# The score-times-value product of a gated linear attention in three fp32r passes instead of one fp32 product

## The chip, the cores and the metric

The kernel runs on one core of one Trainium2 chip. The metric is the time of one execution on the device in microseconds (us), the median of several runs. The profile is one more execution, taken by the hardware profiler. PE is the TensorE, DVE the VectorE, ACT the ScalarE, POOL the GpSimd, and SP the engine that issues most DMAs.

## What is computed

One layer of a decoder trunk on 256 tokens of width 2048, in float32. The normalised input is multiplied by a wide weight matrix. Its columns feed three branches: a causal convolution, a gated linear attention (GLA) and a cross-attention into 256 memory tokens. Each branch is projected back, gated, and the sum goes through an output matrix and a last RMSNorm.

The change is in the GLA. For each of four heads the reference does this, chunk by chunk over the tokens:

```
scores = einsum("bhtk,bhsk,bhtsk->bhts", qi, ki, decay)
o_intra = einsum("bhts,bhsv->bhtv", scores, vi)
o = o_inter + o_intra
```

The kernel does not carry a state. It builds the whole causal 256 x 256 score matrix of a head, decay included, as three blocks of 128 x 128, and multiplies it by v (256 tokens x 512): the first token block from one score block, the second from two.

## The kernel before, in words

**The large products.** All weight products go in three passes of upper and lower parts: a float32 number is split into `hi`, rounded to the PE's short float32 form (fp32r), and `lo`, the rest, also fp32r, and `mm3` (L180 to L183) adds hi x hi, hi x lo and lo x hi. Weights arrive in chunks of two 128-row blocks, 512 KB each; `chunk` (L150) issues the DMA on SP, ACT writes `hi` (L160) and DVE writes `lo` (L161). Four raw buffers and five pairs of hi and lo let this run ahead of the PE. `group_t` (L185) makes 512 output features x 256 tokens with 24 matmuls of 256 columns per chunk, `group_n` (L195) 256 tokens x 512 features with 12 matmuls of 512 columns per chunk.

**The order.** The program runs group after group: the first convolution group (ca0, cb0), q0, k0, va and vb (head 0's v and the small decay input), v1, ca1, cb1, q1, k1, v2, v3, ca2, cb2, mk, mv, mq, mz, then the gate and output groups (gm, ym, gz, go, yo, cz, gc, yc, out). Between chunks `tick` (L117) lets side tasks emit a few instructions: the convolution taps, the norms, and `gla_head` (L517) for each head. A planner then orders each engine's instructions, by its own estimate of durations and by priority, with the weight chunks preferred. On the chip every engine works its list strictly in that order.

**The head.** `gla_head` forms the scores over several levels (`pd`, `pl`), corrects the first block in `sT[:, 0]`, makes the cross block in `px` (L623) and turns the last block around in `pf` (L626). DVE copies those two from PSUM into `sX` (L624) and `s1` (L627). After a pause of two ticks the PE makes `po` (L635, L637, L638): three plain fp32 matmuls of 512 columns per head. ACT sums the squares (L641), POOL the scale, DVE writes the normalised result (L643).

**v.** `v_group` (L666) makes v in one 4 KB tile (per partition) per head; ACT copies it out of PSUM (L671, and L677 and L686 for head 0).

**Pools and offsets.** Tiles of 4 KB come from a pool of NB4 = 19, of 2 KB from NB2 = 7, of 1 KB from NB1 = 8. `KICKS` (L40) lists, per group, chunks whose second row block lies 64 bytes further on in the hi and lo buffers; nothing else depends on it:

```
lines = [1] * (ck - 1) + [2 if k // CK in shifted else 1]
...
first = LINE * at[0]
step = GC + LINE * (at[-1] - at[0])
```

Of the kernel before, what the change touches and what calls it, by code (L numbers as in the profile page):

```python
# [9 lines left out]
F32R = mybir.dt.float32r  # L10
# [6 lines left out]
P = 128  # L17
D = 2048
T = 256
NT = T // P  # L20
# [7 lines left out]
DVH = 512  # L28
# [2 lines left out]
RANK = 16  # L31
MEM_W = 512
MHD = 128
NB4, NB2, NB1, NRAW, NHL = 19, 7, 8, 4, 5
NU, LAG, HELD, XWAIT = 2, 2, 12, 8
WARM = 9
SPARE = 1.2
LINE, HLW = 16, CK * GC + P

KICKS = {"ca0": (0, 4), "cb0": (2,), "ca1": (0,), "cb1": (6,), "q1": (2, 4, 6, 7), "k1": (1, 5), "ca2": (0, 4),  # L40
         "cb2": (0, 3), "mk": (0, 2, 5), "mq": (5,), "mz": (1, 4, 7), "gm0": (0, 2, 3), "go0": (0, 4, 5),
         "go1": (3, 5), "yo1": (6,), "go2": (0,)}
AHEAD = 400
LEVELS = (1, 2, 4, 8, 16, 32, 64)

# [16 lines left out]
def trunk_kernel(ctx, tc, streamed, xt, memt, x, weights, w_alpha2, vecs, taps, b_gate, b_conv_out,  # L62
                 final_g, ident_in, masks_in, out):
    nc = tc.nc
# [6 lines left out]
    def mm_tile(name):  # L71
        return ps.tile([P, GC], F32, name=name, tag="mm", bufs=5)

    def aux_tile(name):
        return ps.tile([P, GC], F32, name=name, tag="aux", bufs=3)

    def b4(shape, name, dt=F32):
        return bp.tile(shape, dt, name=name, tag="b4", bufs=NB4)
# [4 lines left out]
    def t2(shape, name):  # L83
        return tp.tile(shape, F32, name=name, tag="t2", bufs=NB2)

    def t1(shape, name, dt=F32):
        return tp.tile(shape, dt, name=name, tag="t1", bufs=NB1)
# [8 lines left out]
    def start(gen, rank=1):  # L96

        task = [gen, 0, rank]
        at = len(Side.queue)
        while at and Side.queue[at - 1][2] > rank:  # L100
            at -= 1
        Side.queue.insert(at, task)
        return task
# [60 lines left out]
    def chunks(w, cols, nk, acts, name, first=CK, spare=False, shifted=None):  # L164
        if not isinstance(cols, list):
            cols = [(cols, GC)]
        k = 0
        while k < nk:
            ck = min(CK, first) if k < 2 * first else CK
            lines = None  # L170
            if shifted is not None:
                lines = [1] * (ck - 1) + [2 if k // CK in shifted else 1]
            hi, lo = chunk(w, k, ck, cols, f"{name}_{k}", spare and k + ck > nk - HELD and k < nk - 8, lines)
            ops = [acts(k + kk) for kk in range(ck)]
            for kk in range(ck):
                yield k + kk, hi[kk], lo[kk], *ops[kk]
            k += ck
            tick()

    def mm3(o, ah, al, bh, bl, first, last):  # L180
        nc.tensor.matmul(o, lhsT=ah, rhs=bh, start=first, stop=False, skip_group_check=True)  # L181
        nc.tensor.matmul(o, lhsT=ah, rhs=bl, start=False, stop=False, skip_group_check=True)  # L182
        nc.tensor.matmul(o, lhsT=al, rhs=bh, start=False, stop=last, skip_group_check=True)  # L183

    def group_t(w, c0, acts, nk, name, first=CK):  # L185

        pss = [mm_tile(f"pt_{name}_{j}") for j in range(2)]
        for k, hi, lo, ah, al in chunks(w, c0, nk, acts, name, first, shifted=KICKS.get(name, ())):
            for n in range(4):
# [5 lines left out]
    def group_n(w, c0, acts, nk, name):  # L195

        n = sum(c[1] for c in c0) if isinstance(c0, list) else GC
        pss = [mm_tile(f"pn_{name}_{t}")[:, 0:n] for t in range(NT)]
        for k, hi, lo, ah, al in chunks(w, c0, nk, acts, name):
            for t in range(NT):  # L200
                tok = slice(t * P, (t + 1) * P)
                mm3(pss[t], ah[:, tok], al[:, tok], hi, lo, k == 0, k == nk - 1)
        return pss

    def split(src, hi, lo):
        nc.scalar.copy(hi, src)
        nc.vector.tensor_sub(lo, src, hi.bitcast(F32))
# [9 lines left out]
    def rms_scale(ss, n, name, w=1):  # L217

        ms = tp.tile([P, w], F32, name=f"ms_{name}", tag="ms")
        nc.vector.tensor_scalar(ms, ss, 1.0 / n, EPS, op0=ALU.mult, op1=ALU.add)  # L220
        rs = tp.tile([P, w], F32, name=f"rs_{name}", tag="rs")
        nc.gpsimd.tensor_tensor(rs, ms, mhalf[:, 0:w], op=ALU.pow)
        return rs
# [292 lines left out]

    def gla_head(h, q, k, v):  # L517

        while len(cum) <= h:
            yield "wait", 1  # L520
        c = cum[h]
# [12 lines left out]
            return bass.AP(tensor=ap.tensor, offset=ap.offset + at, ap=[list(ap.ap[0]), *(list(x) for x in dims)])  # L534

        sT = t1([P, 2, P], f"sT{h}")
        sX = t1([P, P], f"sX{h}")
        s1 = t1([P, P], f"s1{h}")

        qq = b4([P, 4, P + CHUNK], f"qq{h}")  # L540
        d1 = t1([P, T], f"dq{h}_1")
# [11 lines left out]
        for i in range(2):  # L553
            for a in range(2):
                keys = k[:, a, 0:P] if i == 0 else ck[:, 3 * T + a * P:3 * T + (a + 1) * P]
                nc.tensor.matmul(pdv[:, i, :], lhsT=keys, rhs=qq[:, 2 * a + i, :],
                                 start=a == 0, stop=a == 1, skip_group_check=True)
# [63 lines left out]
        px = aux_tile(f"px{h}")  # L621
        for a in range(2):
            nc.tensor.matmul(px[:, 0:P], lhsT=kd[:, a, :], rhs=qd[:, a, :], start=a == 0, stop=a == 1)  # L623
        nc.vector.tensor_copy(sX, px[:, 0:P])  # L624
        pf = aux_tile(f"pf{h}")
        nc.tensor.matmul(pf[:, 0:P], lhsT=flip, rhs=sT[:, 1, :], start=True, stop=True)  # L626
        nc.vector.tensor_copy(s1, pf[:, 0:P])  # L627
        yield "wait", 2

        ov = b4([P, NT, DVH], f"on{h}")  # L630
        on[h] = ov
        for t in range(NT):
            po = aux_tile(f"po{h}_{t}")
            if t == 0:
                nc.tensor.matmul(po, lhsT=sT[:, 0, :], rhs=v[:, 0, :], start=True, stop=True)  # L635
            else:
                nc.tensor.matmul(po, lhsT=sX, rhs=v[:, 0, :], start=True, stop=False)  # L637
                nc.tensor.matmul(po, lhsT=s1, rhs=v[:, 1, :], start=False, stop=True)  # L638
            sq = t2([P, DVH], f"osq{h}_{t}")
            ss = tp.tile([P, 1], F32, name=f"oss{h}_{t}", tag="ss")  # L640
            nc.scalar.activation(sq, po, AF.Square, accum_out=ss)  # L641
            rs = rms_scale(ss, DVH, f"o{h}_{t}")
            nc.vector.tensor_scalar_mul(ov[:, t, :], po, rs)  # L643
            yield 0.7

    def qk_group(g, acts, rb=None):
        rbb = None if rb is None else rb.unsqueeze(1).to_broadcast([P, 2, T])
        pq = group_t("w_in", C_Q + g * GC, acts, KT, f"q{g}")
        q = b4([P, 4, T], f"q{g}")
        for j in range(2):  # L650
            qj = q[:, 2 * j:2 * j + 2, :]
            if rb is None:
                nc.scalar.activation(qj, pq[j], AF.Copy, scale=DKH ** -0.5)
            else:
                nc.vector.scalar_tensor_tensor(qj, pq[j], DKH ** -0.5, rbb, op0=ALU.mult, op1=ALU.mult)
        pk = group_t("w_in", C_K + g * GC, acts, KT, f"k{g}")
        k = b4([P, 4, T], f"k{g}")
        for j in range(2):
            kj = k[:, 2 * j:2 * j + 2, :]
            if rb is None:  # L660
                nc.scalar.copy(kj, pk[j])
            else:
                nc.vector.tensor_mul(kj, pk[j], rbb)
        return q, k

    def v_group(h, q, k):  # L666
        v = b4([P, NT, DVH], f"v{h}")
        if h:
            pv = group_n("w_in", C_V + h * DVH, X, KT, f"v{h}")
            for t in range(NT):  # L670
                nc.scalar.copy(v[:, t, :], pv[t])  # L671
        else:

            n = (DVH + RANK) // 2
            pv = group_n("w_in", [(C_V, n)], X, KT, "va")
            for t in range(NT):
                nc.scalar.copy(v[:, t, 0:n], pv[t])  # L677
            pv = group_n("w_in", [(C_V + n, DVH - n), (C_AL, RANK)], X, KT, "vb")
            alr = t1([P, NT, P], "alr")
            nc.gpsimd.memset(alr, 0.0)  # L680
            for t in range(NT):
                al = pv[t][:, DVH - n:n]
                nc.scalar.copy(alr[:, t, 0:RANK].bitcast(F32R), al)
                nc.vector.tensor_sub(alr[:, t, 32:32 + RANK].bitcast(F32R), al, alr[:, t, 0:RANK])
                nc.vector.tensor_copy(alr[:, t, 64:64 + RANK], alr[:, t, 0:RANK])
                nc.scalar.copy(v[:, t, n:DVH], pv[t][:, 0:DVH - n])  # L686
            start(decay(alr))
        s = slice(2 * (h % 2), 2 * (h % 2) + 2)
        return start(gla_head(h, q[:, s, :], k[:, s, :], v))


    def memory_groups():
# [172 lines left out]
    q, k = qk_group(0, XR, xrb)  # L865
    finish(norm)
    load_masks()
    gla = [v_group(0, q, k), v_group(1, q, k)]
    tapsk.append(conv_group(1, X))
    q, k = qk_group(1, X)  # L870
    gla += [v_group(2, q, k), v_group(3, q, k)]
    start(load_biases())
    mnorm = start(mem_norm(), rank=0)
# [43 lines left out]
    for n in range(3):  # L917
        po = group_n("w_out", n * GC, Y, KT, f"out{n}")
# [35 lines left out]
    for k, hi, lo, ah, al in chunks("w_out", 3 * GC, KT, Y, "out3", spare=True):  # L954
        mm3(pss[0], ah[:, 0:P], al[:, 0:P], hi, lo, k == 0, k == KT - 1)
        held.append((k, hi, lo, ah, al))
        if k < KT - HELD:
            k, hi, lo, ah, al = held.pop()
# [53 lines left out]
```

## Time and profile before

| what | value |
|---|---|
| median of 3 runs | 1223.62 us (1223.38 to 1223.81) |
| profiled execution, its own time | 1224.49 us |
| span of its instructions | 1222.6 us |
| granted PE clock, mean over the span | 0.999 |
| busy share PE, DVE, ACT, POOL | 99%, 77%, 49%, 2% |

The span is the time from the first to the last instruction; the execution's own time has a little more around it. Starts of matmuls are recorded; their ends are modelled and overlap, so the step from one start to the next, not the duration, is what a matmul costs in a stream. An fp32 matmul stands in the trace as two records.

### The profile page before, as it was taken

Reading aid. Unit: us, or ns where it says so; the run is one execution under the profiler, and the core shown is the slowest. Engines: PE = TensorE matmul, PEld = TensorE weight load, DVE = VectorE, ACT = ScalarE, POOL = GpSimd, SP = SyncE. Lnnn points to the kernel's source line nnn. Section 1 sums busy time; section 2 is a strip of 40 time slices with the busy share of each in tenths; the row PEclk is TensorE's granted clock in tenths of the full one; section 3 lists DMA queues with packets and bytes.
Section 4 is the critical chain, followed back from the end, with each engine's and each line's share of the span. In section 5 each row is a group of like instructions: output and inputs, shape, how many; then the busy total and the mean of one; then the engine's idle time right before and its main releaser. Section 6 shows DMA issues by size and latency. Waiting matters only on the chain.

```text
span 1222.6 us, 22810 instructions
## 1 busy us (share of the span) xinstructions
PE 1210.4 (99%) x9337; PEld 1156.4 (95%) x9337; DVE 938.0 (77%) x1479; ACT 598.1 (49%) x743; POOL 21.6 (2%) x32
## 2 busy tenths in 40 slices
PE   8999999999999999999999999999999999999997
PEld 8999899989998999999988999999999999999885
DVE  6999999699999667997699967974565554555553
ACT  6734666446553454444444445444354544444442
POOL 0000000100030000000000000000000000000000
PEclk9999999999999999999999999999999999999999
DMA  9666756457556545666565665566666666666862
GB/s 339 222 184 191 222 165 205 151 158 236 187 162 199 165 150 178 197 199 194 171 206 187 190 192 156 190 222 191 193 189 204 192 191 195 197 193 204 281 213 78
DMA packets 70488, 236.57 MB, mean 193 GB/s; under 512 B 8192, under 2 KB 12480, under 8 KB 70384
## 3 DMA queue, kind: packets, MB, share of 16 engines
q1 hardware_dynamic: 69952, 234.54, 61.2%
q8 instruction: 73, 1.20, 0.4%
q10 hardware_dynamic: 432, 0.58, 0.1%
q14 instruction: 31, 0.25, 0.1%
HBM read 232.99 MB, written 2.10 MB: 192 GB/s over the span
## 4 chain that ended last, share of the span: by engine, by line
PE 95%; DMA 2%; DVE 2%; issue 0%; ACT 0%; SPq 0%; POOL 0%; POOLq 0%; DVEq 0%; ACTq 0%
PE pt_go L181 2%; PE pt_gm L181 2%; PE pt_go L182 2%; PE pt_go L183 2%; PE pt_cz L182 2%; PE pt_yo L181 2%; PE pn_gz L182 2%; PE pt_yo L182 2%; PE pt_gc L182 2%; PE pn_gz L181 2%; PE pt_yc L183 2%; PE pn_out L181 2%; PE pn_out L183 2%; PE pn_gz L183 2%; PE pt_gm L182 2%; PE pt_yc L182 2%
## 5 line engine op out<-in xcount | busy, mean ns | idle before, releaser
L407 DVE SCALAR_TENSOR_TENSOR conv<-u,tap,conv 128x256 f32<-128x256 f32 x480 | 207.7, 480 | 0.0
L161 DVE TENSOR_TENSOR lo_yc<-raw_yc,hi_yc 128x1024 fp32r<-128x1024 f32 x32 | 39.2, 1226 | 47.6 <-ACT hi_yc L160 47.6
L181 PE MATMUL pt_ca<-xh,hi_ca 128*128 128x256 f32 x256 | 70.6, 279 | 1.5 <-ACT hi_ca L160 1.5
L181 PE MATMUL pt_go<-xh,hi_go 128*128 128x256 f32 x256 | 71.4, 279 | 0.0
L182 PE MATMUL pt_gm<-xl,hi_gm 128*128 128x256 f32 x256 | 71.2, 278 | 0.0
L183 PE MATMUL pt_gm<-xh,lo_gm 128*128 128x256 f32 x256 | 71.2, 278 | 0.0
L181 PE MATMUL pt_cb<-xh,hi_cb 128*128 128x256 f32 x256 | 71.0, 279 | 0.0
L183 PE MATMUL pt_go<-xh,lo_go 128*128 128x256 f32 x256 | 71.0, 277 | 0.0
L182 PE MATMUL pt_go<-xl,hi_go 128*128 128x256 f32 x256 | 71.0, 277 | 0.0
L181 PE MATMUL pt_yo<-oh,hi_yo 128*128 128x256 f32 x256 | 70.9, 277 | 0.0
L183 PE MATMUL pt_ca<-xh,lo_ca 128*128 128x256 f32 x256 | 70.2, 278 | 0.7 <-DVE lo_ca L161 0.7
L182 PE MATMUL pt_ca<-xl,hi_ca 128*128 128x256 f32 x256 | 70.7, 278 | 0.2 <-DVE xl L211 0.2
L181 PE MATMUL pt_gm<-xh,hi_gm 128*128 128x256 f32 x256 | 70.8, 277 | 0.0
L182 PE MATMUL pt_yo<-ol,hi_yo 128*128 128x256 f32 x256 | 70.8, 277 | 0.0
L183 PE MATMUL pt_yo<-oh,lo_yo 128*128 128x256 f32 x256 | 70.8, 276 | 0.0
L182 PE MATMUL pt_gc<-xl,hi_gc 128*128 128x256 f32 x256 | 70.8, 276 | 0.0
L181 PE MATMUL pt_yc<-uh,hi_yc 128*128 128x256 f32 x256 | 70.8, 276 | 0.0
L183 PE MATMUL pt_yc<-uh,lo_yc 128*128 128x256 f32 x256 | 70.8, 276 | 0.0
L181 PE MATMUL pt_gc<-xh,hi_gc 128*128 128x256 f32 x256 | 70.8, 276 | 0.0
L183 PE MATMUL pt_cz<-xh,lo_cz 128*128 128x256 f32 x256 | 70.7, 276 | 0.0
L183 PE MATMUL pt_gc<-xh,lo_gc 128*128 128x256 f32 x256 | 70.7, 276 | 0.0
L182 PE MATMUL pt_yc<-ul,hi_yc 128*128 128x256 f32 x256 | 70.7, 276 | 0.0
(354 smaller groups left out, 4410.5 us busy)
## 6 DMA issues: line engine op xcount, KB each, us to landing
raw_cb<-in_weights SPq DMA_DIRECT2D x32, 512.0 KB, 4.4
raw_gm<-in_weights SPq DMA_DIRECT2D x32, 512.0 KB, 3.6
raw_gz<-in_weights SPq DMA_DIRECT2D x32, 512.0 KB, 4.0
raw_go<-in_weights SPq DMA_DIRECT2D x32, 512.0 KB, 4.1
raw_yo<-in_weights SPq DMA_DIRECT2D x32, 512.0 KB, 4.0
raw_cz<-in_weights SPq DMA_DIRECT2D x32, 512.0 KB, 4.2
raw_gc<-in_weights SPq DMA_DIRECT2D x32, 512.0 KB, 3.5
raw_yc<-in_weights SPq DMA_DIRECT2D x32, 512.0 KB, 3.9
```

The lines of the kernel that those rows point to most:

```text
L161: nc.vector.tensor_sub(lo, raw, hi.bitcast(F32))
L181: nc.tensor.matmul(o, lhsT=ah, rhs=bh, start=first, stop=False, skip_group_check=True)
L182: nc.tensor.matmul(o, lhsT=ah, rhs=bl, start=False, stop=False, skip_group_check=True)
L183: nc.tensor.matmul(o, lhsT=al, rhs=bh, start=False, stop=last, skip_group_check=True)
L407: nc.vector.scalar_tensor_tensor(acc, u[:, i, j:j + T], tap[:, i, j:j + 1], acc, op0=ALU.mult, op1=ALU.add)
```

## The change

The scores and v are split into upper and lower parts, and the fp32 matmuls of `po` become `mm3`. `sX` and `s1` are now written by ACT (upper) and DVE (lower) instead of one DVE copy; the first score block, used in place before, gets such a split too, into a new tile `s0`. v has two 4 KB tiles, and after ACT's copy out of PSUM DVE computes the lower part. The 4 KB pool grows by one tile, the 2 KB pool loses two. The list `KICKS` changes for seven groups.

```diff
-NB4, NB2, NB1, NRAW, NHL = 19, 7, 8, 4, 5
+NB4, NB2, NB1, NRAW, NHL = 20, 5, 8, 4, 5
-KICKS = {"ca0": (0, 4), "cb0": (2,), "ca1": (0,), "cb1": (6,), "q1": (2, 4, 6, 7), "k1": (1, 5), "ca2": (0, 4),
-         "cb2": (0, 3), "mk": (0, 2, 5), "mq": (5,), "mz": (1, 4, 7), "gm0": (0, 2, 3), "go0": (0, 4, 5),
-         "go1": (3, 5), "yo1": (6,), "go2": (0,)}
+KICKS = {"ca0": (0, 4), "cb0": (2,), "ca1": (0,), "cb1": (6, 7), "q1": (3, 5, 7), "k1": (0, 2, 3, 4, 5),
+         "ca2": (0, 4), "cb2": (0, 2), "mk": (0,), "mq": (0, 1, 2, 3, 5), "mz": (1, 4, 7), "gm0": (0, 2, 3),
+         "go0": (0, 4, 5), "go1": (3, 5), "yo1": (6,), "go2": (0,)}
...
-        sX = t1([P, P], f"sX{h}")
-        s1 = t1([P, P], f"s1{h}")
+        s0, sX, s1 = (t1([P, 2, P], f"{n}{h}", F32R) for n in ("s0", "sX", "s1"))
...
-        nc.vector.tensor_copy(sX, px[:, 0:P])
+        split(px[:, 0:P], sX[:, 0, :], sX[:, 1, :])
...
-        nc.vector.tensor_copy(s1, pf[:, 0:P])
+        split(pf[:, 0:P], s1[:, 0, :], s1[:, 1, :])
+        split(sT[:, 0, :], s0[:, 0, :], s0[:, 1, :])
...
-            if t == 0:
-                nc.tensor.matmul(po, lhsT=sT[:, 0, :], rhs=v[:, 0, :], start=True, stop=True)
-            else:
-                nc.tensor.matmul(po, lhsT=sX, rhs=v[:, 0, :], start=True, stop=False)
-                nc.tensor.matmul(po, lhsT=s1, rhs=v[:, 1, :], start=False, stop=True)
+            for n, (sn, vt) in enumerate(((s0, 0),) if t == 0 else ((sX, 0), (s1, 1))):
+                mm3(po, sn[:, 0, :], sn[:, 1, :], v[0][:, vt, :], v[1][:, vt, :], n == 0, n == t)
...
-        v = b4([P, NT, DVH], f"v{h}")
+        vh, vl = (b4([P, NT, DVH], f"{n}{h}", F32R) for n in ("vh", "vl"))
...
-                nc.scalar.copy(v[:, t, :], pv[t])
+                split(pv[t], vh[:, t, :], vl[:, t, :])
...
-                nc.scalar.copy(v[:, t, 0:n], pv[t])
+                split(pv[t], vh[:, t, 0:n], vl[:, t, 0:n])
...
-                nc.scalar.copy(v[:, t, n:DVH], pv[t][:, 0:DVH - n])
+                split(pv[t][:, 0:DVH - n], vh[:, t, n:DVH], vl[:, t, n:DVH])
```

`split` and `mm3` exist already:

```
def split(src, hi, lo):
    nc.scalar.copy(hi, src)
    nc.vector.tensor_sub(lo, src, hi.bitcast(F32))
```

## Rows read from the trace of the kernel before

**Rows 1.** The page: busy time by engine, and the chain that ended last, by engine

```profile
PE 1210.4 (99%) x9337; PEld 1156.4 (95%) x9337; DVE 938.0 (77%) x1479; ACT 598.1 (49%) x743; POOL 21.6 (2%) x32
...
PE 95%; DMA 2%; DVE 2%; issue 0%; ACT 0%; SPq 0%; POOL 0%; POOLq 0%; DVEq 0%; ACTq 0%
```

**Rows 2.** Waits of PE, two of the five: us in total, times, longest

```profile
PE pt_ca L181 <- ACT hi_ca L160: 1.5, 1, 1.5
...
PE pt_q L183 <- DVE lo_q L161: 0.6, 1, 0.6
```

**Rows 3.** Timeline of PE in group k1, head 0: start us, us, engine, line

```profile
220.23 1.02 PE L637 MATMUL po<-v,sX 128*128 128x512 f32 x2
221.09 1.02 PE L638 MATMUL po<-v,s 128*128 128x512 f32 x2
221.94 0.61 PE L566 MATMUL pl<-d 128*128 128x128 f32 x4
```

**Rows 4.** Timeline of PE in an undisturbed 512-column stream, 22 steps

```profile
1129.99 0.39 PE L181 MATMUL pn_out<-hi_out,yh 128*128 128x512 f32 x1
...
1134.98 0.39 PE L182 MATMUL pn_out<-lo_out,yh 128*128 128x512 f32 x1
```

**Rows 5.** Timeline of PE in group mq: 11 steps, fp32 px, 22 steps

```profile
395.83 0.28 PE L182 MATMUL pt_mq<-xl,hi_mq 128*128 128x256 f32 x1
...
397.07 0.28 PE L181 MATMUL pt_mq<-xh,hi_mq 128*128 128x256 f32 x1
397.19 0.61 PE L623 MATMUL px<-qd,kd 128*128 128x128 f32 x4
...
397.75 0.28 PE L183 MATMUL pt_mq<-xh,lo_mq 128*128 128x256 f32 x1
...
400.34 0.28 PE L181 MATMUL pt_mq<-xh,hi_mq 128*128 128x256 f32 x1
```

**Rows 6.** Timeline of PE in group mz, chunk 1 and after: 26 steps, 22 steps

```profile
418.98 0.28 PE L182 MATMUL pt_mz<-xl,hi_mz 128*128 128x256 f32 x1
...
422.06 0.28 PE L181 MATMUL pt_mz<-xh,hi_mz 128*128 128x256 f32 x1
...
424.56 0.28 PE L182 MATMUL pt_mz<-xl,hi_mz 128*128 128x256 f32 x1
```

**Rows 7.** Timeline of PE after 512-column groups: ca1, 25 steps; mq, 10 steps

```profile
143.49 0.28 PE L181 MATMUL pt_ca<-xh,hi_ca 128*128 128x256 f32 x1
...
146.44 0.28 PE L182 MATMUL pt_ca<-xl,hi_ca 128*128 128x256 f32 x1
...
389.34 0.28 PE L181 MATMUL pt_mq<-xh,hi_mq 128*128 128x256 f32 x1
...
390.47 0.28 PE L182 MATMUL pt_mq<-xl,hi_mq 128*128 128x256 f32 x1
```

**Rows 8.** Groups of instructions: count, busy us, mean ns, idle us before

```profile
L207 DVE TENSOR_TENSOR yl<-y,yh 128x512 fp32r<-128x512 f32 x8 | 5.5, 687 | 0.0
...
L624 DVE COPY sX<-px 128x128 f32<-128x128 f32 x4 | 1.1, 287 | 1.9 <-PE px L623 1.7
...
L671 ACT COPY v<-pn_v 128x512 f32<-128x512 f32 x6 | 3.4, 580 | 2.4 <-PE pn_v L183 2.4
```

**Rows 9.** Windows: stretch, us, busy us of PE, PEld, DVE, ACT, POOL; PE clock

```profile
97.00:415.00 318.00, 318.00 (x2310) 297.04 (x2309) 298.75 (x589) 175.22 (x226) 15.18 (x12) 1.00 0.59 186
415.00:598.00 183.00, 183.00 (x1583) 181.97 (x1583) 143.53 (x234) 83.66 (x105) 0.00 (x0) 1.00 0.61 185
```

**Rows 10.** Timelines of DVE and PE where v1 begins

```profile
119.21 1.22 DVE L161 TENSOR_TENSOR lo_v<-raw_v,hi_v 128x1024 fp32r<-128x1024 f32 x1
...
120.90 0.39 PE L182 MATMUL pn_v<-lo_v,xh 128*128 128x512 f32 x1
```

**Rows 11.** Timeline of ACT in k1, [idle before <- releaser]

```profile
218.28 1.05 ACT L160 CAST hi_k<-raw_k 128x1024 fp32r<-128x1024 f32 x1 [3.71 <-PE pt_k L182]
```

**Rows 12.** Windows: from the end of the memory branch to gz

```profile
455.50:598.00 142.50, 142.50 (x1258) 142.47 (x1257) 117.86 (x192) 62.40 (x70) 0.00 (x0) 1.00 0.64 193
```

More of the change, by code (lines that the diff above doesn't have):

```diff
@@ L685, in v_group @@
                 nc.vector.tensor_copy(alr[:, t, 64:64 + RANK], alr[:, t, 0:RANK])
-                nc.scalar.copy(v[:, t, n:DVH], pv[t][:, 0:DVH - n])
+                split(pv[t][:, 0:DVH - n], vh[:, t, n:DVH], vl[:, t, n:DVH])
             start(decay(alr))
         s = slice(2 * (h % 2), 2 * (h % 2) + 2)
-        return start(gla_head(h, q[:, s, :], k[:, s, :], v))
+        return start(gla_head(h, q[:, s, :], k[:, s, :], (vh, vl)))
     def memory_groups():
```

## The prediction

> **What bounds the kernel.** I read the page first: the PE is busy for 1210.4 of 1222.6 us, and the chain that ended last is 95% PE [rows 1]. The list of the PE's waits comes next: the longest is 1.5 us, in the first group, and the latest in time is 0.6 us in q0; behind that the PE waits for no other engine [rows 2]. So from q0 on the time is the sum of the steps between matmul starts, and only what changes that sum, or makes the PE wait anew, moves the end. The windows show what cover the others have: over 97 to 415 us, where all GLA work lies, the PE is busy throughout at a granted clock of 1.00 (the 2.4 GHz level), DVE for 298.75 of 318 us and ACT for 175.22 [rows 9]. DVE has 19 us of room there, ACT 143.
>
> The steps were read from timelines. In an undisturbed 512-column fp32r stream 22 steps take 4.99 us, 0.2268 each [rows 4]. An fp32 matmul of `po` takes 0.86 and 0.85 us from its start to the next start, 0.855 on the mean [rows 3]. A 256-column stream has **two steps, a short and a long one**: in mq 11 steps take 1.24 us (0.1127) before the fp32 product px and 22 steps take 2.59 us (0.1177) behind it [rows 5]. The long undisturbed stretch before gz gives 142.5 us for 1258 matmuls, 0.1133 [rows 12], so the long step costs 0.0044 us a matmul, or 0.105 us a chunk of 24. It does not end by itself within such a run: in mz, behind another fp32 product, 26 steps take 3.08 us (0.1185), and then 22 take 2.50 (0.1136) [rows 6]. The turn comes just behind chunk 1, a chunk that `KICKS` names for mz. That is what the 64-byte offsets do.
>
> **The change, part by part.**
>
> 1. *The products.* Three fp32 matmuls per head become nine fp32r ones, in the same places of the program. Removed: 12 x 0.855 = 10.26 us. Added: 36 x 0.2268 = 8.16 us. Gain 2.10 us, all of it on the PE's own path. The step of a lone fp32r triple between 256-column matmuls is not in the trace. It is bounded below by 0.214, the half of an fp32 record (0.855 / 4, which is 512 columns at 2.4 GHz), and above by 0.2268 x 0.1177 / 0.1133 = 0.2356, if the long step applies to it in full. That makes the gain 1.78 to 2.57 us. I take 0.2268, since only that row is of the same type and width. The Trainium skill, "TensorE: Matmul & The Clock Gate", section "Back-to-back issue gap", gives N/2.4 + 2.5 ns for an isolated warm matmul, 215.8 ns at 512 columns, whatever the type; by it the gain would be 12 x (0.855 - 3 x 0.2158) = 2.49 us. This trace does not agree for fp32r: 226.8 ns.
>
> 2. *The offsets.* From cb1 to mq the old list names 13 chunks and the new one 18; outside those groups nothing changes. They end stretches of long steps, and these begin at products put between the large matmuls. The change has as many of them as before, twelve, but of another type. Whether fp32r of 512 columns turns the step when 256-column matmuls follow, two places leave open: behind v1 (with four 256-column fp32r matmuls last) ca1 has long steps, 25 in 2.95 us (0.118), and behind mv mq has short ones, 10 in 1.13 us [rows 7]. Bounds: if the five further chunks are five more of long steps, they cost 5 x 0.105 = 0.5 us; if each of the old 13 stood for one such chunk and all went, 13 x 0.105 = 1.4 us are gained. I take 0, because the number of interruptions stays, and keep both ends.
>
> 3. *DVE.* v's lower parts: six of 128 x 512, nearest row 687 ns, and four of half that, taken at 0.4 us: 4.1 + 1.6 = 5.7 us. Per head three subtractions of 128 x 128 come and two copies go (287 ns each): +0.29, 1.1 us for four heads [rows 8]. Together 6.9 us, hidden by the 19 us of room up to 415 and, for what slips further, the 39 us that DVE idles from 415 to 598 [rows 9]; the convolution taps are what gives way. If the cover fails, a weight chunk's `lo` is late and the PE waits. The closest call is v1's second chunk step: `lo` done at 119.21 + 1.22 = 120.43, used at 120.90 [rows 10]. The 0.47 us of slack stand right behind va's eviction, where the change puts two subtractions (0.8 us). At nothing if the planner takes two taps less there, 0.4 us if it doesn't; I take 0.
>
> 4. *ACT and the new hand-over.* ACT copies v as before (580 ns). New are three small casts per head, below 580 ns each [rows 8], 7 us at most in 143 us of idle time. But `po` now waits for px -> ACT -> DVE instead of px -> DVE, and ACT's list is strict: in head 0 ACT stood 3.71 us before a weight cast because its buffer was still in use by the PE, and then worked 1.05 us on it [rows 11]. A cast of sX queued behind that is late, and so is the subtraction behind it on DVE, with the weight chunk's `lo` queued behind that. The two ticks of pause before `po` (two chunks, 48 x 0.1133 = 5.4 us) cover it. Nothing taken; up to 1.05 + 0.29 + 0.29 = 1.6 us for one head where they don't.
>
> 5. *Pools.* Two heads' v are alive at once, so two more 4 KB tiles have one more place, and the levels and evictions share five 2 KB tiles instead of seven. Late next would be a head's level tiles and the memory branch's operands. Neither is waited for by the PE in [rows 2], and the heads are due only at gz (598 us). Nothing taken; the price of a miss is in the new-waits rival. No DMA on SP or work on POOL is added or moved.
>
> Sum: -2.10. The profiled execution would go from 1224.49 to 1222.4 us (span 1222.6 to 1220.5); the median stands 0.87 us below the profiled execution, so 1223.62 - 2.10 = **1221.5 us**. A measurement of this kernel can tell about 0.2%, 2.45 us, from no change: faster means below 1221.17.
>
> **The rivals.**
>
> *Fewer long steps.* fp32 is what turned the step, in px and in mz [rows 5, 6]; with fp32r in `po` and offsets at more chunks, some long stretches vanish. For: mv to mq stays short [rows 7]. Against: ca1 does not. Of the 1.4 us some 1.2 us gained: 1220.3 us.
>
> *Passes at the fp32 rate.* The PE moves an fp32 record at 0.214 per 512 columns [rows 3]; should the inserted triples run so, the gain is 2.57 us and the time 1221.05. Against it stand 22 even steps at 0.2268 [rows 4]. The skill's 215.8 ns, quoted above, would come out nearly there.
>
> *New waits.* The late casts of point 4 or the slack of point 3 make the PE wait, 0.4 to 1.6 us, say 1.5 in sum: 1223.0 us. Against: before, no wait in GLA's stretch.
>
> *Long steps handed on (the other side).* The offsets of mz and gm0 are unchanged and bring back the short step by the end of gm0. If they turn the step over rather than set it, and mq now ends with the other one, the stream leaves gm0 with long steps, and no offset follows before gz: 1258 matmuls [rows 12] x 0.0044 = 5.5 us, 1223.62 - 2.10 + 5.5 = 1227.0 us. It decides as soon as more than 2.10 / 0.0044 = 480 further matmuls take the long step. Against: the new list has its five further chunks close to mq.
>
> **How the numbers follow.** Main case 0.50, fewer long steps 0.32, passes at the fp32 rate 0.05, new waits 0.07, long steps handed on 0.06. Faster by over 0.2%: 0.32 + 0.05 + 0.03 from the main case's lower end (a gain of over 2.45 us) = 0.40. Slower by over 0.2%: 0.06. Within: 0.54. The main case's own range is 1221.0 (gain 2.57) to 1222.3 (gain 1.78, offsets +0.5). The range given, 1219.7 to 1223.6, takes in most of the fewer-long-steps case (its end is 2.57 + 1.4 = 3.97, 1219.65) and the new waits; it leaves out the long steps handed on.
>
> **What would show it.** In the trace after, each `po` start should stand 3 x 0.2268 = 0.68 us before the next foreign matmul's; 0.64 or 0.71 means the bounds of point 1. The PE's waits should still list none behind q0; a wait of `po` on DVE would be the new-waits case. 192 matmuls of gm1 at 0.1133 say that no long step was handed on; in k1, mk and mq the long stretches should number about as before. The prediction is wrong if the PE's stretch from 165 to 415 us shrinks by much more or less than 2.1 us.

## The result and the profile after

The changed kernel takes 1231.31 us (1229.91 to 1231.90, 6 runs), the kernel before beside it 1224.35 (6 runs): a ratio of 1.0056, interval 1.0047 to 1.0066. Slower by 7 us, where 1221.5 with an upper end of 1223.6 was forecast. The profiled execution took 1231.46 us, its span is 1229.6. Executions of one kernel lie in groups some 1.6 us apart (of 25 of the kernel before, 13 took 1223.4 to 1224.7 and 12 took 1225.1 to 1226.5), so a difference of under 1 us between medians of few runs says little.

First the busy times and the chain of the page, against [rows 1]:

```profile
PE 1213.8 (99%) x9349; PEld 1162.9 (95%) x9349; DVE 943.4 (77%) x1493; ACT 600.0 (49%) x755; POOL 13.9 (1%) x32
...
PE 92%; DVE 4%; DMA 2%; issue 0%; ACT 0%; POOL 0%; SPq 0%; POOLq 0%; DVEq 0%; ACTq 0%
```

DVE has twice its share of the chain. The PE's waits say where (compare [rows 2]); total, times, longest:

```profile
PE bc_m L231 <- DVE dg_m L230: 3.4, 1, 3.4
PE pt_ca L181 <- ACT hi_ca L160: 1.5, 1, 1.5
...
PE pt_q L183 <- DVE lo_q L161: 0.6, 1, 0.6
...
PE pl L566 <- DVE sT L568: 0.5, 1, 0.5
```

bc_m is the memory branch's: it spreads the 256 tokens' norm scales, made from the row sums pq_m by fs_m (PE), rs_m (POOL) and dg_m (DVE), over the partitions, and only then can mk leave PSUM (L695; L700 in the kernel before). Windows over that place, columns as in [rows 9]:

```profile
389.00:392.40 3.40, 3.40 (x30) 3.22 (x28) 3.40 (x8) 0.00 (x0) 0.00 (x0) 1.00 0.63 190
392.40:395.80 3.40, 0.05 (x2) 0.06 (x1) 2.81 (x10) 0.00 (x0) 2.39 (x1) 0.85 0.31 118
395.80:398.00 2.20, 2.20 (x10) 2.20 (x11) 2.20 (x10) 0.50 (x2) 0.00 (x0) 0.50 0.00 0
398.00:400.30 2.30, 1.85 (x8) 1.30 (x6) 2.30 (x9) 0.97 (x2) 0.00 (x0) 0.50 0.00 0
400.30:403.20 2.90, 2.86 (x12) 2.65 (x13) 2.90 (x8) 0.00 (x0) 0.00 (x0) 0.50 0.00 0
403.20:405.00 1.80, 1.80 (x10) 1.80 (x10) 1.65 (x6) 0.00 (x0) 0.20 (x1) 0.50 0.09 15
405.00:407.00 2.00, 2.00 (x19) 2.00 (x18) 0.30 (x1) 1.05 (x1) 0.00 (x0) 0.99 0.07 18
```

The PE stands still for 3.4 us, and for the 9.2 us behind that the granted clock is 0.50, which is 1.2 GHz. The Trainium skill, "TensorE: Matmul & The Clock Gate", section "HAM oscillation — how this bites in real kernels", describes the like for waits on a DMA: a PE that idles while it waits for its operands starts the next burst at half clock. The trace agrees: 0.50 behind the gap, 1.00 ahead of it.

mz starts at 422.27 us instead of 415.28. That is the whole loss; the long stretch behind it [rows 12] is the same to the hundredth:

```profile
462.49:604.99 142.50, 142.50 (x1258) 142.47 (x1257) 117.85 (x192) 62.38 (x70) 0.00 (x0) 1.00 0.64 193
```

The account of the 6.99 us goes by steps from start to start. Between mq's last start ahead of the gap, at 392.14, and 405.06 us, where the steps are short again, 12.92 us pass over 37 matmuls. At the 0.113 us of the full clock these take 4.2, so 8.7 are lost: 3.5 in the wait at bc_m, and 5.2 at half clock, with the second wait of 0.5 inside. This execution also lost some 0.2 before va. The products gained 1.8: 36 steps from a `po` start to the next start add up to 8.45 us, against the 10.26 of before. 8.7 + 0.2 - 1.8 = 7.1. The passes in the timeline of the PE, head 1's nine between 512-column matmuls:

```profile
247.68 0.40 PE L181 MATMUL po<-vh,s 128*128 128x512 f32 x1
...
249.55 0.40 PE L183 MATMUL po<-vh,s 128*128 128x512 f32 x1
249.79 0.39 PE L182 MATMUL pn_v<-lo_v,xh 128*128 128x512 f32 x1
```

Nine passes in 2.11 us, 0.2344 each.

**Why bc_m is late.** Each of the four memory operands arrives in one 4 KB tile, is squared on ACT, summed on DVE, and split into two more such tiles, `mh` and `ml`. In the kernel before the last split (`ml`, L211) is done by 329 us, fs_m runs at 356.8 and bc_m at 374.2, inside mv. Groups of the tile ml and of fs_m: durations min/median/max in ns, first and last start, before:

```profile
L211 DVE SCALAR_TENSOR_TENSOR ml<-mr,vec,mh x16: 466/467/470, 295.7 to 328.6; 128x256 fp32r<-128x256 f32 x16
...
L239 PE MATMUL fs_m<-ones,pq_m x4: 164/250/251, 356.8 to 357.1; 128*128 128x1 f32 x4
```

And after:

```profile
L211 DVE SCALAR_TENSOR_TENSOR ml<-mr,vec,mh x16: 476/496/499, 298.4 to 361.0; 128x256 fp32r<-128x256 f32 x16
...
L239 PE MATMUL fs_m<-ones,pq_m x4: 164/250/250, 389.3 to 389.5; 128*128 128x1 f32 x4
```

Both are 32 us late. By the program's addresses the last `ml` lies in the place of the first `mh`, and the trace has it written right behind mh's last use, at 359.9. Two more of the 4 KB places than before are held at that time, by the second v tiles of heads 2 and 3 (first written at 268.8 and 293.2 us), and the pool has one more. From fs_m to bc_m, in the timelines of DVE, POOL and PE:

```profile
392.61 0.15 DVE L220 TENSOR_SCALAR ms_m<-fs_m 128x2 f32<-128x2 f32 x1
392.91 2.39 POOL L222 TENSOR_TENSOR rs_m<-ms_m,mhalf 128x2 f32<-128x2 f32 x1 [10.87 <-DVE ms_m L220]
395.33 0.48 DVE L230 TENSOR_SCALAR dg_m<-idents,rs_m 128x128 f32<-128x128 f32 x2 [0.59 <-POOL rs_m L222]
395.77 0.77 PE L231 MATMUL bc_m<-dg_m,ones 128*128 128x128 f32 x2 [3.35 <-DVE dg_m L230]
```

ms_m stands behind other work in DVE's list for 2.8 us after fs_m is done, and POOL's step takes 2.39 us (0.80 in e13_hold_s0 and e4_oldkicks). From 359 us to ms_m neither DVE nor the PE stands still for the late operand. Its lateness is in the order that the planner gave their lists, and shows as a wait only at bc_m. The PE meanwhile runs ahead into mq. Mk's two PSUM tiles still stand, and by the addresses mq's second tile lies in the place of mk's first. So when the 60 matmuls of mq's first tile are through, the PE has nothing left but bc_m.

### The profile page after: what moved, and what is told of

The parts are those of the page before. It is cut to its first block, busy times and chain, and to the rows that moved or that the text cites. A ratio compares the mean times of both kernels' runs of the same rounds, so it can differ in the third digit from the quotient of the medians.

```text
span 1229.6 us, 22865 instructions
## 1 busy us (share of the span) xinstructions
PE 1213.8 (99%) x9349; PEld 1162.9 (95%) x9349; DVE 943.4 (77%) x1493; ACT 600.0 (49%) x755; POOL 13.9 (1%) x32
## 4 chain that ended last, share of the span: by engine, by line
PE 92%; DVE 4%; DMA 2%; issue 0%; ACT 0%; POOL 0%; SPq 0%; POOLq 0%; DVEq 0%; ACTq 0%
PE pt_go L181 2%; PE pt_yo L181 2%; PE pt_go L182 2%; PE pt_go L183 2%; PE pt_yc L182 2%; PE pt_gc L182 2%; PE pt_gm L183 2%; PE pt_cz L181 2%; PE pn_gz L182 2%; PE pt_gm L181 2%; PE pn_gz L181 2%; PE pn_gz L183 2%; PE pn_out L181 2%; PE pt_gm L182 2%; PE pn_out L183 2%; PE pt_yo L183 2%
## 5 line engine op out<-in xcount | busy, mean ns | idle before, releaser
L181 PE MATMUL pt_cz<-xh,hi_cz 128*128 128x256 f32 x256 | 70.7, 276 | 0.0
L182 PE MATMUL pt_cz<-xl,hi_cz 128*128 128x256 f32 x256 | 70.7, 276 | 0.0
```

## The experiments

All are compared with runs of the kernel before on the same chip. A first theory was the 4 KB places; what was left over from it led to the second.

**Sizes of the pools and the offsets.**

```diff
# e1_pools, the kernel before
-NB4, NB2, NB1, NRAW, NHL = 19, 7, 8, 4, 5
+NB4, NB2, NB1, NRAW, NHL = 20, 5, 8, 4, 5
# e2_before18, the kernel before
+NB4, NB2, NB1, NRAW, NHL = 18, 7, 8, 4, 5
# e3_after21, the changed kernel
+NB4, NB2, NB1, NRAW, NHL = 21, 3, 8, 4, 5
# e4_oldkicks, the changed kernel with the list of the kernel before
-KICKS = {... "k1": (0, 2, 3, 4, 5), ... "mq": (0, 1, 2, 3, 5), ...}
+KICKS = {... "k1": (1, 5), ... "mq": (5,), ...}
```

> The kernel before with 20 tiles of 4 KB and 5 of 2 KB, nothing else changed. Theory (the loss comes from the 4 KB pool being short by one once v has two tiles a head, so the memory branch is late and the PE waits for the broadcast of its row scale): here nothing is short, the broadcast is made inside mv as before, no new PE wait, time within 1.2 us of the kernel before. Rival (two fewer 2 KB tiles delay the heads and through them the memory branch): some us slower, with a PE wait on the broadcast.

1224.78 against 1224.38, ratio 1.0000 (0.9991 to 1.0010). The pools' new sizes cost nothing while v has one tile.

> The kernel before with 18 tiles of 4 KB instead of 19, nothing else changed: short by one without any of the change's arithmetic. Theory (4 KB pool): the last memory operand waits for a place, mk and mv get interleaved, the row-scale broadcast slips into mq, and the PE waits some us for it with the clock falling after: 4 to 9 us slower, 1228 to 1233. Rival (2 KB pool, casts or offsets): no more than 1.5 us slower.

1226.17, ratio 1.0009 (1.0000 to 1.0019). The memory operands are as late as in the changed kernel, the last `ml` at 363.6 us, and still the PE waits only 0.2 us there. Too high an expectation: lateness is not yet a wait.

> The changed kernel with 21 tiles of 4 KB and 3 of 2 KB. Theory (4 KB pool): the memory branch is on time, no PE wait beyond the first us of the kernel, granted clock 0.999, and the products' gain of 2.1 us shows: 1220.5 to 1224, that is 7 to 10 us below the changed kernel. Rival (the casts of the hand-over through ACT, or the new offsets, cause the loss): it stays at 1229 to 1232. Rival (2 KB pool): worse than the changed kernel.

1229.86, ratio 1.0042 (1.0026 to 1.0059). With a 21st place the last `ml` comes at 336.5 and the wait at bc_m is gone. The time did not follow: two waits in q1 have come in, where three 2 KB tiles are left (e8_before21_3 tests that):

```profile
PE pt_q L181 <- ACT sg L388: 2.0, 1, 2.0
PE pl L566 <- DVE sT L568: 1.4, 1, 1.4
```

> The changed kernel with the list of offsets of the kernel before. Theory (4 KB pool): the wait and the lower clock stay, the time is 1230 to 1234, since the offsets can only move the long steps, some 0.1 us a chunk. Rival (the new offsets cause the loss): 1225 or less.

1229.67, ratio 1.0047 (1.0030 to 1.0064). In the profiled execution (1233.42 us) the waits are there with the old offsets (bc_m 2.6, pl 2.9 us in three), and so is the half clock. The offsets are not the cause. The median is 1.6 us below the changed kernel's, and the two intervals overlap.

**The second tile, and what pays for places.**

```diff
# e5_novl: the changed kernel without v's lower tile
-        vh, vl = (b4([P, NT, DVH], f"{n}{h}", F32R) for n in ("vh", "vl"))
+        vh = b4([P, NT, DVH], f"vh{h}", F32R)
-                split(pv[t], vh[:, t, :], vl[:, t, :])
+                nc.scalar.copy(vh[:, t, :], pv[t])
...
-                mm3(po, sn[:, 0, :], sn[:, 1, :], v[0][:, vt, :], v[1][:, vt, :], n == 0, n == t)
+                nc.tensor.matmul(po, lhsT=sn[:, 0, :], rhs=v[:, vt, :], start=n == 0, stop=False, skip_group_check=True)
+                nc.tensor.matmul(po, lhsT=sn[:, 1, :], rhs=v[:, vt, :], start=False, stop=n == t, skip_group_check=True)
# e7_raw3: the changed kernel
-NB4, NB2, NB1, NRAW, NHL = 20, 5, 8, 4, 5
+NB4, NB2, NB1, NRAW, NHL = 21, 5, 8, 3, 5
# e8_before21_3: the kernel before
-NB4, NB2, NB1, NRAW, NHL = 19, 7, 8, 4, 5
+NB4, NB2, NB1, NRAW, NHL = 21, 3, 8, 4, 5
```

> The changed kernel without v's lower tile: po is made of two passes (both parts of the scores times v's upper part), and the product of the scores with v's lower part is left out. Everything else, pools and offsets too, is as in the changed kernel. Theory (the second 4 KB tile per head keeps the memory operands out of the pool, and bc_m is late): two places in 4 KB come free from 267 us on, ml3 gets its place about as early as in the kernel before, bc_m stands inside mv, and the PE's waits list neither bc_m nor a half clock. Against the kernel before it then gains 12 x 0.855 - 24 x 0.2268 = 4.8 us: 1218 to 1221. Rival (the strict hand-over px, ACT, DVE delays DVE and with it the memory branch): the three casts and subtractions of each head are still there, so the wait of about 3 us and the half clock stay: 1231.3 - 2.7 = about 1228.5.

1219.76 against 1224.20, ratio 0.9961 (0.9946 to 0.9976): 4.4 us faster, where the theory had 4.8, with no wait behind q0, the last `ml` split by 322 and fs_m at 363.4. The casts and subtractions of the score splits are all still in; only v's lower tile, its subtractions and its 12 passes are out.

> The changed kernel with 21 tiles of 4 KB and all five tiles of 2 KB, paid for by one raw weight buffer (three instead of four). Theory: as in the earlier run with 21 tiles the bc_m wait goes, and this time the levels keep their five 2 KB tiles, so the waits of q1 go too: 1221 to 1224, unless three raw buffers let the PE wait for weights, which the list of its waits would show as waits on hi or lo. Rival (lateness is DVE's load): bc_m wait stays, 1229 to 1232.

1245.08, ratio 1.0170 (1.0154 to 1.0185). No wait at bc_m, but weights come late from the first group on:

```profile
PE pt_ca L181 <- ACT hi_ca L160: 3.7, 3, 1.6
PE pt_ca L183 <- DVE lo_ca L161: 3.7, 4, 1.9
PE pt_cb L183 <- DVE lo_cb L161: 3.5, 3, 2.1
```

With weights so late, its silence on bc_m proves little. It says what a raw buffer is worth: 13.8 us against the changed kernel, 20.9 against the kernel before.

> The kernel before with 21 tiles of 4 KB and only three of 2 KB. It measures what three 2 KB tiles cost by themselves. If the waits of q1 in the earlier run of the changed kernel with 21 and 3 (2.0 and 1.4 us, then the half clock) come from the three 2 KB tiles, they are here too, and the time is 4 to 8 us above the kernel before. If they come from the work that the change adds, none is here and the time is that of the kernel before within 1 us.

1227.35, ratio 1.0023 (1.0012 to 1.0033): waits of 0.8 and 0.6 us at the same two lines of q1. So the three 2 KB tiles alone cost 3 us, and part of the stalls of e3_after21 is theirs.

**The same work, another order.**

```diff
# e6_v3late: the changed kernel
-    gla += [v_group(2, q, k), v_group(3, q, k)]
+    gla.append(v_group(2, q, k))
...
     tapsk.append(conv_group(2, X))
+    gla.append(v_group(3, q, k))
# e10_memfirst: the changed kernel
-    gla += [v_group(2, q, k), v_group(3, q, k)]
+    gla.append(v_group(2, q, k))
...
     mnorm = start(mem_norm(), rank=0)
+    gla.append(v_group(3, q, k))
# e11_v3late_q0k0: e6_v3late; e12_before_q0k0: the kernel before
-KICKS = {... "cb0": (2,), ...}
+KICKS = {... "cb0": (2,), "q0": (1,), "k0": (1,), ...}
```

> The changed kernel with one group moved: v3 comes behind ca2 and cb2 instead of right behind v2. Head 3's two v tiles then take their places some 70 us later. Theory (places in 4 KB held by v2 and v3 at once): the memory operands get their places before the PE needs bc_m, no wait at bc_m and no half clock; against the changed kernel 7 us or more come back: 1221 to 1224.5, at best the kernel before less 2.1 us. A new wait may come at the end, since head 3 is finished later, though its result is due only at gz, 598 us in the kernel before. Rival (the loss comes from more work on DVE, whatever the places): the work is the same, so the wait stays, 1229 to 1232.

1224.51 against 1224.20, ratio 0.9999 (0.9989 to 1.0009). All of the change's work is in, fs_m is at 332.0 and bc_m at 346.8, and the list of waits has nothing behind q0. The 7 us are back, the products' 1.8 are not won: in the profiled execution q0 and k0 took the long step, 382 matmuls with 1.64 us above the short one, which the profile of before did not.

> The changed kernel with two statements exchanged: the memory branch's norm is started before v3 is asked for, so its operands stand ahead of head 3's two v tiles in the line for places. Groups, products, offsets and pools are those of the changed kernel. Theory: fs_m and bc_m come back into mk, no wait and no half clock; head 3 ends later, in mz, which nothing awaits before gz: 1221.5 to 1224.5. Rival (the DVE's load): the same work in the same groups keeps the memory branch late, 1229 to 1232.

1226.33 against 1224.29, ratio 1.0017 (1.0008 to 1.0026). fs_m is back at 337.1 and bc_m at 350.4. The time is above the range given; what the longer executions lose is not shown. In the profiled one (1224.88 us) head 3 ends late enough to delay the memory values, and mz waits for them:

```profile
PE pt_mz L181 <- ACT mv L699: 1.9, 1, 1.9
```

> The run with v3 behind ca2 and cb2, with a 64-byte offset also at chunk 1 of q0 and of k0. In the profile of that run without these offsets the 382 matmuls of q0 and k0 took the long step behind the PE's wait for lo_q (1.64 us above 0.1133 each); in the profile of the kernel before they took the short one behind the same wait. Theory: which step follows the wait differs from execution to execution, and an offset brings the short one back within a chunk or two: q0 and k0 at 0.1133 but for 24 to 48 matmuls, and a median 0.4 to 1.5 us below that run's 1224.5. Rival: the offset turns the step over, so that executions that had the short step get the long one: the median stays within 0.3 us or rises by up to 1.6.

1223.08 against 1224.29, ratio 0.9989 (0.9981 to 0.9998), its 11 runs within 1222.91 to 1223.99. **This is the one full version that beats both kernels, the one before by 0.1%.** Timeline of the PE over k0, first in e6_v3late:

```profile
76.74 0.28 PE L181 MATMUL pt_k<-xh,hi_k 128*128 128x256 f32 x1
...
99.35 0.28 PE L181 MATMUL pn_va<-hi_va,xh 128*128 128x264 f32 x1
```

and here:

```profile
75.75 0.28 PE L181 MATMUL pt_k<-xh,hi_k 128*128 128x256 f32 x1
...
97.57 0.29 PE L181 MATMUL pn_va<-hi_va,xh 128*128 128x264 f32 x1
```

k0's 192 steps take 22.61 us, 0.1178 each; with the offsets 21.82, 0.1136.

> The kernel before with the same two offsets, at chunk 1 of q0 and of k0, as the control of the run before it. Theory (the offset sets the short step): the kernel before, whose executions mostly have the short step there, gains 0 to 0.6 us. Rival (the offset turns the step over): q0 and k0 have the long step for part or all of their length, and the time rises by 0.5 to 1.6 us.

1224.13 against 1224.29, ratio 1.0000 (0.9991 to 1.0009). No loss, so the offset does not turn a short step over; no gain either, as the theory's lower end has it.

**What turns late operands into a wait.** e2_before18 had the lateness without the wait, so the tile alone was tried, in the kernel before.

```diff
# e9_hold: the kernel before, NB4 = 20, NB2 = 5
+            if t:
+                nc.vector.tensor_mul(vl[:, 0, 1:2], po[:, 0:1], vl[:, 0, 0:1])
...
-        v = b4([P, NT, DVH], f"v{h}")
+        v, vl = (b4([P, NT, DVH], f"{n}{h}") for n in ("v", "vl"))
...
+        nc.scalar.copy(vl[:, 0, 0:1], v[:, 0, 0:1])
# e13_hold_s0: e9_hold; e14_s0: the kernel before
+        s0 = t1([P, P], f"s0{h}")
...
         nc.vector.tensor_copy(s1, pf[:, 0:P])
+        nc.vector.tensor_copy(s0, sT[:, 0, :])
...
-                nc.tensor.matmul(po, lhsT=sT[:, 0, :], rhs=v[:, 0, :], start=True, stop=True)
+                nc.tensor.matmul(po, lhsT=s0, rhs=v[:, 0, :], start=True, stop=True)
# e15_t0plain: the changed kernel
-        s0, sX, s1 = (t1([P, 2, P], f"{n}{h}", F32R) for n in ("s0", "sX", "s1"))
+        sX, s1 = (t1([P, 2, P], f"{n}{h}", F32R) for n in ("sX", "s1"))
...
-        split(sT[:, 0, :], s0[:, 0, :], s0[:, 1, :])
...
+            if t == 0:
+                nc.tensor.matmul(po, lhsT=sT[:, 0, :], rhs=v[0][:, 0, :].bitcast(F32), start=True, stop=True)
...
```

> The kernel before, fp32 products and old offsets, with 20 and 5 tiles in the pools, and a second 4 KB tile for each head that holds nothing of use: ACT writes one column of it after v, and one DVE instruction of one column reads it behind po. No pass, split or subtraction of the change is in it. Theory (the places alone): the memory operands come late as in the changed kernel, the PE waits at bc_m or right behind it by 2 to 4 us and then runs some microseconds at half clock: 1229 to 1233. Rival (DVE's 6.9 us more work and the hand-over over ACT are needed too): no wait of over 1 us at bc_m, 1224 to 1226.5.

1224.60 against 1224.29, ratio 1.0005 (0.9996 to 1.0014). **The first theory falls as it stood**: the last `ml` comes at 361.7, as late as in the changed kernel, and the PE does not wait. The rows show what is different: fs_m runs at 380.41, 9 us sooner.

```profile
338.85 1.02 PE L635 MATMUL po<-v,sT 128*128 128x512 f32 x2
...
380.41 0.50 PE L239 MATMUL fs_m<-ones,pq_m 128*128 128x1 f32 x4
...
391.77 0.38 PE L231 MATMUL bc_m<-dg_m,ones 128*128 128x128 f32 x2
```

Head 2's first `po` stands at 338.85: it reads the score block in place. In the changed kernel it needs the new split s0, and that stands in DVE's list behind the reduction of the late operand (timeline of DVE, changed kernel):

```profile
366.37 2.03 DVE L250 TENSOR_REDUCE pq_m<-mr 128x256 f32<-128x1024 f32 x1
368.32 0.28 DVE L207 TENSOR_TENSOR sX<-px,sX 128x128 fp32r<-128x128 f32 x1
...
369.11 0.28 DVE L207 TENSOR_TENSOR s<-sT,s 128x128 fp32r<-128x128 f32 x1
...
385.56 0.74 DVE L641 TENSOR_SCALAR on<-po,rs_o 128x512 f32<-128x512 f32 x1
386.45 0.73 DVE L641 TENSOR_SCALAR on<-po,rs_o 128x512 f32<-128x512 f32 x1
```

So both `po` of head 2 come at 368 and 374 and leave PSUM only at 386 to 387, and fs_m, at 389.3, comes behind that. By the program's addresses fs_m lies in the PSUM place of the first of them, as it does in e9_hold, where that `po` is out by 370.1. The PE does not stand still before fs_m, so the place acts through the planner's order.

> The kernel before with the idle second 4 KB tile per head (20 and 5 tiles in the pools) and one thing more: the first score block is no longer used in place, one DVE copy of 128 x 128 (about 0.29 us, four in all) puts it into s0 behind the copy of s1, and po's first matmul reads s0. Theory (place and copy together): the copies stand behind the late memory reduction in DVE's list, po_0 comes some 30 us later, the PSUM places of po and pd come free later and fs_m with them, at 388 to 390 us instead of 380; the PE waits 2 to 4 us at bc_m and runs at half clock behind it: 1229 to 1234. Rival (the passes, v's subtractions or ACT's casts are needed): 1224 to 1226.5, no wait of over 1 us at bc_m.

1226.31 against 1224.66, ratio 1.0015 (1.0006 to 1.0025). fs_m is where the theory puts it, but bc_m costs little:

```profile
389.89 0.50 PE L239 MATMUL fs_m<-ones,pq_m 128*128 128x1 f32 x4
...
394.97 0.46 PE L231 MATMUL bc_m<-dg_m,ones 128*128 128x128 f32 x2 [0.16 <-DVE dg_m L230]
```

One tile and one copy of 0.22 us bring the whole lateness, bc_m at 395.0 against 395.8. What is missing is the PE's side: here it is through with mq's 60 matmuls at 394.7, in the changed kernel at 392.3, for the passes had by then won it 1.4 us (three heads of four), and this execution had the long step in q0 and k0, some 0.9 us by va. The expected time was too high by that. What stays above the kernel before is 1.65 us; the profile has waits of 0.2 and 0.6 us here, and the long step.

> The kernel before, its pools too (19 and 7), with the copy of the first score block into s0 alone: the control of the run beside it. Theory: without the second tile the memory operands are in time, DVE's copies are not held up, and nothing waits: 1224 to 1225.5. Rival (the copy alone delays the memory branch): a wait at bc_m and 1229 to 1234 here too.

1225.05, ratio 1.0003 (0.9994 to 1.0013): fs_m at 359.5, no new wait. The copy alone does nothing.

> The changed kernel, its places, its v in two tiles, its splits of sX and s1 and its offsets, but po's first matmul reads the first score block in place, in one fp32 product with v's upper tile; the product of the first block with v's lower part is left out, and s0 and its split are gone. In products that is 4 x (0.855 - 3 x 0.235) = 0.6 us more than the changed kernel. Theory: po_0 comes early again, at about 340 us, fs_m at 379 to 382 though the memory operands are as late as in the changed kernel; the wait at bc_m is under 1 us and there is no half clock: 1231.3 - 8.4 + 0.6 = 1223.5, 1222 to 1225. Rival (the late places alone, with any of the change's other work): the wait stays, 1230 to 1233.

1225.90, ratio 1.0010 (1.0000 to 1.0019), 0.9 us above the range; the profiled execution took 1224.71. `po` is at 338.35 again, fs_m at 379.68 and bc_m at 390.77 with no wait before it, though the last `ml` is as late as ever. Left are two smaller waits behind it, 1.2 us in sum, of `pl` for DVE's correction of sT; its windows keep the clock at 1.00:

```profile
391.00:394.00 3.00, 2.62 (x23) 2.42 (x22) 3.00 (x12) 0.42 (x1) 0.00 (x0) 1.00 0.58 175
394.00:397.00 3.00, 2.08 (x14) 1.72 (x15) 3.00 (x10) 0.94 (x2) 0.20 (x1) 1.00 0.06 6
```

So the whole loss came only with three things together, and each of them has been left out once: the tile in e5_novl, s0 in e15_t0plain, the passes with their splits in e13_hold_s0. In the kernel before, the tile alone gives 1224.60, tile and s0 1226.31, tile, s0 and the passes with their other splits (e4_oldkicks) 1229.67. From the changed kernel, taking out the tile gives 1219.76, taking out s0 1225.90, and moving v3 1224.51. Two limits: the third thing is a bundle, and that the PE's earlier arrival is the part of it that counts, and not DVE's further subtractions, is argued from the times above; and each edit made the planner order the lists anew, so a run shows an edit with its new order.

## Why the prediction was wrong

**The step that failed is point 5, the pools, together with point 4, the hand-over.** Point 5 counted the places right (two more tiles, one more place) and named the memory branch's operands as what would be late next, and then took nothing, since no wait for them stood in [rows 2]. But that list shows only what is late already. The slack was to be had from the trace of before: bc_m at 374.2 stands 15 us ahead of the start of mq, and in the changed kernel the PE had nothing else left at 392.3, 18 us later. The operands came 32 us late. Alone this moved bc_m to 391.8 and cost no wait (e9_hold); with s0 and the passes it came at 395.8, and the PE waited.

Point 4 looked at sX, where two chunks of pause cover it. The part that mattered was s0: before, the first score block was used in place, and po_0 did not depend on what stood in DVE's list behind it. e15_t0plain shows what that was worth.

**The price of a miss** was mis-sized too. The new-waits rival, with 7 chances in 100, had waits of 1.5 us in sum and no loss of clock; measured were 3.9 us of waits and 4.7 of half clock.

**Point 1, the products**, was right in sign and mis-sized by 0.3 us: 0.2344 to 0.235 a pass, its upper bound (0.2356), not the 0.2268 taken. The gain is 1.8 us. The 215.8 ns that point 1 quotes from the Trainium skill, by a formula that names no data type, do not hold for these passes either. **Point 2, the offsets**: nothing, as taken; between 165 and 430 us the long steps cost 2.4 us with the old list and 2.3 with the new one. (The list changes for six groups, not seven; with ca2, which stays, it names 15 and 20 chunks from cb1 to mq. The difference of five stands.) **Point 3, DVE**: its busy time grew by 5.4 us instead of 6.9 (938.0 to 943.4), and no weight came late for it; the harm was in its order. **Long steps handed on**, the rival that was to end slower, did not happen: the 142.50 us above.

## What to carry to other kernels

A pool's new tile is priced by walking to the next tenant: which load gets its place later, what chain hangs on it, and how far that chain's end stands ahead of the PE. An empty list of waits is not that distance. A value that was used in place and now needs an instruction on a strict queue is a new dependency, whatever the instruction's length. And where a side chain sets the moment, a faster main stream only arrives at the wait sooner: here that is 1.4 of the 3.4 us.

## What the runs showed of the hardware

- Not every gap costs the clock. Behind 3.4 us of idle PE the granted clock was 0.50 for 9.2 us; in e4_oldkicks it stayed at 1.00 behind a wait of 2.6 and fell to 0.50 behind two more, of 1.3 and 1.0 us; in e3_after21 it fell for 3.4 us behind waits of 1.4 and 2.0. In the profiled execution of e10_memfirst it stayed at 1.00 behind 1.9 us, and in that of e15_t0plain behind two of 1.2 us in sum.
- Which step q0 and k0 take differs from profile to profile, also where nothing of those groups was changed: long in the profile of e14_s0, short in those of e9_hold and of the kernel before. It is worth 1.6 us, more than the 0.1% to which most of these ratios are known, and in e11_v3late_q0k0 an offset at one chunk of each group ended the long stretch.
